# Two transformer blocks with experts: row factors applied late at two steps, narrow FFN ups, second-block projections by rows

## The chip, the cores and the metric

The kernel runs on one core of a Trainium2 chip. The metric is the device time of one execution in microseconds; where several executions are given, their median. The engines have short names in the profile: PE is TensorE (matmuls), DVE VectorE, ACT ScalarE, POOL GpSimd, SP SyncE, whose queue starts the weight transfers.

## What is computed

For 256 tokens of width 1024, all in fp32, two blocks follow one another; x is the residual stream. Cut to the parts that the change touches:

```python
# first block
z = rmsnorm(x, norm1_g) @ w_in + b_in            # attention and a convolution branch follow
x = x + merged @ w_out                           # "wo"
h2 = rmsnorm(x, norm2_g)
up = dwconv(h2 @ w_up) + b;  gate, val = split(up)
x = x + (gelu(gate) * val) @ w_down              # FFN, width 2816
x = rmsnorm(x, norm_f_g)
# second block
h = rmsnorm(x, norm1_gain)
aq, ak, av, mq, mk, mv, mi, mf, mo, gate_a, gate_m = split(h @ w_in)
att = sliding_window_attention(rope(rmsnorm(aq)), rope(rmsnorm(ak)), av)
hm = rmsnorm(mlstm_chunkwise(mq, mk, mv, mi, mf), ml_gain) * sigmoid(mo)
mixed = sigmoid(gate_a) * (att @ w_a) + sigmoid(gate_m) * (hm @ w_m)
x = x + mixed @ w_out                            # "wo2"
q = rmsnorm(x, norm2_gain) @ peer_w_query        # "pq", expert queries
x = x + experts(q, x)                            # 16384 experts, top 16 of 8 heads
```

`rmsnorm(x, g)` is x times g times one factor per token, 1/sqrt(mean(x*x) + eps).

## The kernel before

**Precision.** Every fp32 operand of a matmul is split into a rounded part (h) and a rest (l), and a product is three matmuls: h with h, l with h, h with l.

**Granules.** The weights come in 455 granules of 128 x 1024 numbers. `granule` (L223) starts a 512 KB transfer to a `raw` tile (four of them) on SP's queue, lets ACT round it into `wh` (L238) and DVE subtract the rest into `wl` (L239), three tiles each; then PE reads both. 199 granules are sections of one packed array (`B.sec(name, i)`), 256 are experts.

**Three forms of a granule's matmuls.** `mm_cols` (L255, lines L261 to L263): the weight is stationary, the activations (128 x 256 tokens) move; 24 matmuls of 256 columns, the result has features on partitions. `mm_wide` (L265, L274) moves h and l of the activations side by side: 8 matmuls of 512 and 8 of 256 columns, and `wide_sum` adds the halves with an ACT copy and a DVE add. `mm_rows` (L281, L290 to L292): the activations are stationary, 512 weight columns move; 12 matmuls for the two tiles of 128 tokens, the result has tokens on partitions.

**Norms.** `scaled_cols` (L334) multiplies a tile of tokens by its row factor and by the gain (`nrm`, DVE L341), and `turn` (L353) transposes it on PE in blocks of 128 x 128 (L357) and splits the result into the tiles X that the matmuls read. The row factor needs the whole row: the eviction of the matmul result, a square with sum on ACT, a sum on DVE (L331), a power on POOL (L312). This stands between wo and the FFN (`rows_out`, L679), between the FFN and the second block (L663 to L675, two norms in a row with factors r1 and r3), and between wo2 and pq. There the second half of the columns is done for token tile 0 first, then for tile 1.

**FFN.** For each of 22 slices f two wide up granules fill PSUM banks, a three-tap convolution and gelu run on ACT and DVE, and `down` (L608) adds gh and gl times the third granule to four banks, two f's later; the last downs wait until after the loop, ordered so that half rows end one after the other.

**Second block.** Keys and values (akv), gates (L814), aq and mv are done by rows or cols in `stream1` (L801); mq and mk by cols. Then `drive` runs three generators beside one another: `stream2` (mo, ga2, gm2 by cols, tanh on ACT into so, ta, tb), `attention` (first `qk_norm`, L919, with the rotation on POOL, L936 to L938) and `mlstm` (first `gates`, L854, a scan on DVE). Then ba and bm, the two branch matrices, by cols; their products with the gates are the mixed rows in Y, which wo2 reads. pq by cols gives the expert queries with features on partitions.

**Order.** The program's order is only a first one: a list scheduler sets the order on each engine ahead of time from dependences and its own costs, and each engine then runs its queue in that order. So DVE instructions of the gates and norms stand between wl subtractions.

Of the kernel before, what the change touches and what calls it, by code (L numbers as in the profile page):

```python
# [11 lines left out]
F32 = mybir.dt.float32  # L12
# [39 lines left out]
def _col(v):  # L52
# [4 lines left out]
         ("cb", 4), ("lg", 4), ("lb", 4), ("fw", 132), ("fb", 44), ("mg", 8), ("gb", 1))  # L57
_ROWS = (("n1", D), ("n2", D), ("nf", D), ("m1", D), ("m2", D), ("b_v", 512), ("qg", 64), ("kg", 64),
# [20 lines left out]
def pack(inputs):  # L79
# [105 lines left out]
class Block:  # L185
# [69 lines left out]
    def mm_cols(self, out, w, x, nk, first=True, last=True, off=0):  # L255

        wh, wl = (t[:, off:off + nk * P].rearrange("p (k n) -> p k n", n=P) for t in w)
        xh, xl = x
        mm = self.nc.tensor.matmul
        for k in range(nk):  # L260
            mm(out, wh[:, k], xh[:, k], start=(first and k == 0), stop=False)  # L261
            mm(out, wh[:, k], xl[:, k], start=False, stop=False)  # L262
            mm(out, wl[:, k], xh[:, k], start=False, stop=(last and k == nk - 1))  # L263
# [79 lines left out]

    def warm(self, n):
# [20 lines left out]
def first_block(B, rp):  # L365
    tc, nc, A = B.tc, B.nc, B.A
    with ExitStack() as es:
# [226 lines left out]
        g2 = B.gain(rp, "n2", "gain")  # L594
        X = B.xcol()
        x1 = rows_out(B, rp, "wo", M, x0, 0.5, g2, X, pool,
                      ("qT", "kT", "v", "y", "th", "sig", "oh", "ol"))


    with ExitStack() as es:  # L600
# [3 lines left out]
        late = []  # L604
        acc = [B.bank("at") for _ in range(4)]
# [9 lines left out]

        for f in range(NFF):
# [733 lines left out]
```

## Time and profile before

| | |
|---|---|
| median of 3 runs | 1445.74 us (1445.27 to 1446.1) |
| the profiled execution's own time | 1447.32 us |
| its span, first to last instruction | 1445.5 us |
| mean granted clock of PE in it | 0.993 |
| PE busy | 1423.3 us, 98% of the span |
| DVE, ACT, POOL busy | 1126.8, 766.7, 52.6 us |

By place in the span: first block to the end of wo, 0 to 192 us; FFN to 385; akv and gates to 400; aq, mq, mk, mv to 466; the three generators to 586; ba to 606; bm to 631; wo2 to 652; pq 660 to 682; experts to the end. The times of the rows below are of this one execution. PE's matmuls are pipelined: the duration of one is longer than the distance to the next one's start, so the price of a matmul is read from starts. A granted clock of 1.00 is 2.4 GHz, 0.50 is 1.2 GHz.

### The profile page before, as it was taken

The numbers are of one execution on the slowest core, as the hardware profiler recorded it, in microseconds if no ns is written. First come the engines' busy times: TensorE is split into PE (matmuls) and PEld (weight loads), VectorE is DVE, ScalarE is ACT, GpSimd is POOL, SyncE is SP. The second block draws the span as 40 slices with busy tenths as digits, with TensorE's granted clock in tenths as the row PEclk, the third lists the DMA queues.
The fourth block names the chain that finished last, engine by engine and source line by source line (L and its number), as shares of the span: only waits on it lengthen the run. The fifth ranks groups of instructions, "written<-read, shape, count | busy, mean of one in ns | idle before, by whom it ended". The sixth has DMA issues, their size and how long they took to land.

```text
span 1445.5 us, 24810 instructions
## 1 busy us (share of the span) xinstructions
PE 1423.3 (98%) x9487; PEld 1252.9 (87%) x9487; DVE 1126.8 (78%) x2125; ACT 766.7 (53%) x1225; POOL 52.6 (4%) x97
## 2 busy tenths in 40 slices
PE   8999999999899999999999999999999999999998
PEld 6988978888788988988999999888888888888887
DVE  6997878888797567674997977999969999666665
ACT  5456566667554666454454444555554444455453
POOL 1000000000204000001000000000000000000000
PEclk9999999999999999999999999999999999999999
DMA  7643556556366423474455555555565545555553
GB/s 270 189 137 117 180 168 196 190 187 219 122 188 206 139 96 117 146 242 150 149 174 177 164 191 173 173 164 171 165 211 179 170 168 173 191 191 192 197 193 131
DMA packets 70103, 251.33 MB, mean 174 GB/s; under 512 B 8025, under 2 KB 8417, under 8 KB 69730
## 3 DMA queue, kind: packets, MB, share of 16 engines
q1 hardware_dynamic: 69698, 249.17, 52.3%
q8 instruction: 74, 1.21, 0.3%
q10 hardware_dynamic: 288, 0.59, 0.1%
q14 instruction: 43, 0.35, 0.1%
HBM read 247.63 MB, written 2.11 MB: 173 GB/s over the span
## 4 chain that ended last, share of the span: by engine, by line
PE 91%; DVE 5%; DMA 1%; ACT 1%; issue 1%; POOL 0%; SPq 0%; POOLq 0%; ACTq 0%; DVEq 0%
PE mm L274 19%; PE mm L261 10%; PE mm L262 10%; PE mm L263 10%; PE mm L1293 8%; PE mm L1295 8%; PE mm L1294 8%; PE mm L292 2%; PE mm L291 2%; PE mm L290 2%; PE at L1271 2%; DVE wl L239 2%; PE at L612 1%; PE at L614 1%; PE at L613 1%; DMA raw<-in_ws_dram 1%
## 5 line engine op out<-in xcount | busy, mean ns | idle before, releaser
L239 DVE TENSOR_TENSOR wl<-raw,wh 128x1024 fp32r<-128x1024 f32 x454 | 554.4, 1223 | 159.7 <-ACT wh L238 154.9
L238 ACT ACTIVATE wh<-raw 128x1024 fp32r<-128x1024 f32 (+1 forms) x457 | 479.8, 1051 | 272.6 <-PE mm L262 209.0
L261 PE MATMUL mm<-x,wh 128*128 128x256 f32 x1088 | 312.6, 287 | 1.3 <-ACT wh L238 0.8
L263 PE MATMUL mm<-x,wl 128*128 128x256 f32 x1088 | 310.7, 286 | 2.7 <-DVE wl L239 2.7
L262 PE MATMUL mm<-x,wh 128*128 128x256 f32 x1088 | 311.6, 286 | 0.3 <-DVE x L250 0.2
L274 PE MATMUL mm<-x,wh 128*128 128x512 f32 x864 | 305.2, 399 | 0.0
L274 PE MATMUL mm<-x,wl 128*128 128x256 f32 x864 | 225.0, 281 | 0.0
L261 PEld LDWEIGHTS mm<-x,wh 128*128 128x128 f32 x1088 | 210.4, 193 | 6.5 <-issue 2.9
L263 PEld LDWEIGHTS mm<-x,wl 128*128 128x128 f32 x1088 | 210.3, 193 | 4.4 <-DVE wl L239 3.1
L262 PEld LDWEIGHTS mm<-x,wh 128*128 128x128 f32 x1088 | 210.2, 193 | 3.7 <-issue 2.7
L1293 PE MATMUL mm<-wh,wsh 128*128 128x512 f32 x512 | 201.6, 394 | 0.0
L1295 PE MATMUL mm<-wh,wsl 128*128 128x512 f32 x512 | 199.4, 389 | 0.0
L1294 PE MATMUL mm<-wl,wsh 128*128 128x512 f32 x512 | 199.2, 389 | 0.0
L274 PEld LDWEIGHTS mm<-x,wh 128*128 128x128 f32 x864 | 158.5, 189 | 29.6 <-DVE x L250 0.2
L274 PEld LDWEIGHTS mm<-x,wl 128*128 128x128 f32 x864 | 163.5, 189 | 8.6 <-DVE wl L239 0.2
L249 ACT ACTIVATE wsh<-W 128x256 fp32r<-128x256 f32 x128 | 53.4, 418 | 188.3 <-PE mm L1294 188.0
L1295 PEld LDWEIGHTS mm<-wh,wsl 128*128 128x128 f32 x512 | 96.1, 188 | 20.3
L1294 PEld LDWEIGHTS mm<-wl,wsh 128*128 128x128 f32 x512 | 96.2, 188 | 19.3
L1293 PEld LDWEIGHTS mm<-wh,wsh 128*128 128x128 f32 x512 | 96.2, 188 | 18.9
L250 DVE TENSOR_TENSOR wsl<-W,wsh 128x256 fp32r<-128x256 f32 x128 | 54.2, 424 | 49.4 <-ACT wsh L249 49.3
L278 ACT ACTIVATE W<-mm 128x256 f32<-128x256 f32 x64 | 24.5, 383 | 94.9 <-PE mm L274 94.9
L292 PE MATMUL mm<-wh,x 128*128 128x512 f32 (+1 forms) x160 | 62.0, 387 | 1.3 <-DVE x L250 1.3
(345 smaller groups left out, 1837.4 us busy)
## 6 DMA issues: line engine op xcount, KB each, us to landing
raw<-in_ws_dram SPq DMA_DIRECT2D x199, 512.0 KB, 3.6
raw<-in_pd_dram SPq DMA_DIRECT2D x128, 512.0 KB, 3.5
raw<-in_pu_dram SPq DMA_DIRECT2D x128, 512.0 KB, 3.5
bias<-in_rpb_dram SPq DMA_DIRECT2D x2, 1024.0 KB, 8.5
x<-in_x_dram SPq DMA_DIRECT2D x4, 256.0 KB, 3.6
r_m<-in_rows_dram SPq DMA_DIRECT2D x2, 512.0 KB, 4.7
mb<-negm_d SPq DMA_DIRECT2D x4, 256.0 KB, 5.1
x<-xn SPq DMA_DIRECT2D x2, 512.0 KB, 5.6
```

The lines of the kernel that those rows point to most:

```text
L238: nc.scalar.activation(wh[:, c], raw[:, c], AF.Copy)
L239: eng.tensor_sub(wl[:, c], raw[:, c], wh[:, c].bitcast(F32))
L249: self.nc.scalar.activation(h, src, AF.Copy)
L250: self.nc.vector.tensor_sub(l, src, h.bitcast(F32))
L261: mm(out, wh[:, k], xh[:, k], start=(first and k == 0), stop=False)
L262: mm(out, wh[:, k], xl[:, k], start=False, stop=False)
L263: mm(out, wl[:, k], xh[:, k], start=False, stop=(last and k == nk - 1))
L274: mm(o, a, b, start=(k == 0 and j == 0), stop=(k == 7 and j == 1))
L292: mm(outs[i], xl[:, k0 + k, ts], wh[:, k], start=False, stop=en)
L1293: nc.tensor.matmul(a, wp[0][:, ts], u[0][:, ns], start=(i == 0), stop=False)
L1294: nc.tensor.matmul(a, wp[0][:, ts], u[1][:, ns], start=False, stop=False)
L1295: nc.tensor.matmul(a, wp[1][:, ts], u[0][:, ns], start=False, stop=(i == NE - 1))
```

## The change

Eight things are edited together.

1. Between wo and the FFN and between the FFN and the second block, the activations are multiplied by the gain only (`plain_cols`) and transposed; the row factor is applied to the results. For the FFN it is laid along the free axis (`across`: two matmuls, an ACT copy) and multiplied in the eviction of an up. In the second block it is a scale of ACT's evictions (`full`, `half`) or, for features on partitions, the tile rb again (gates, mq, mk, now evicted on DVE).
2. The ups are 24 narrow matmuls in place of 16 wide ones. Both halves of an f share one bank and one eviction. The first granules of f = 0, 1, 2 are done for the first half of K, then for the second. The FFN's X are two tiles of their own.
3. mo, ga2, gm2, ba, bm and pq use `mm_rows`. hn is multiplied by so before it is transposed; the mixed rows are transposed into Y, 16 blocks; the queries are transposed, 16 blocks.
4. The gain `mg` is a broadcast row, a transfer on SP's queue, instead of a column.
5. pq's first three granules are done for tile 0, then for tile 1.
6. `qk_norm` and `gates` run in a `drive` beside a new generator `stream1b` (mq, mk, mv); their transposes come later, in `qk_cols` and `gate_cols`.
7. The rotation moves from POOL to DVE, the swapped keys from POOL to ACT, y2's scaling from POOL to ACT; akv's evictions go from DVE to ACT.
8. The first granule of aq is done between the akv matmuls of tile 1.

```diff
     def mm_cols(self, out, w, x, nk, first=True, last=True, off=0, k0=0):
...
-            mm(out, wh[:, k], xh[:, k], start=(first and k == 0), stop=False)
+            mm(out, wh[:, k], xh[:, k0 + k], start=(first and k == 0), stop=False)
...
+    def plain_cols(self, pool, src, g, x, k0, i, width=512):
+        for c in range(0, 512, width):
+            ns = slice(k0 * P + c, k0 * P + c + width)
+            y = pool.tile([P, width], F32, tag="nrm", name="nrm", bufs=4)
+            self.nc.vector.tensor_tensor(y, src[:, ns], g[:, ns], op=OP.mult)
+            self.turn(y, x, k0 + c // P, width // P, i)
+    def across(self, pool, rp, r, tag):
...
+        for i in range(2):
+            nc.vector.tensor_copy(w[:, i:i + 1], bc(r[i], P))
+        b = self.bank("at")
+        for i in range(2):
+            nc.tensor.matmul(b[:, i * P:(i + 1) * P], w[:, i], self.ident, start=True, stop=True)
+        rb = pool.tile([P, T], F32, tag=tag, name="rb")
+        nc.scalar.activation(rb, b[:, 0:T], AF.Copy, scale=32.0)
+        return rb
...
+        rb = B.across(pool, rp, r1, "rb")
...
+        ahead = [B.sec("ffn", 3 * f) for f in range(3)]
+        for kh in range(2):
+            for f, w in enumerate(ahead):
...
+                B.mm_cols(ups[f][:, 0:T], w, X, 4, kh == 0, kh == 1, kh * 512, 4 * kh)
         for f in range(NFF):
+            b = ups.get(f) or B.bank("mm")
+            for j in range(2):
+                if j or f not in ups:
+                    B.mm_cols(b[:, j * T:(j + 1) * T], B.sec("ffn", 3 * f + j), X, 8)
...
+            nc.vector.tensor_tensor(u[:, :, 1:T + 1], b.rearrange("p (a t) -> p a t", a=2), bc_at(rb, 1, 2),
+                                    op=OP.mult)
...
-                b = B.bank("mm")
-                B.mm_wide(b, B.sec("ffn", 3 * f + j), X)
-                B.wide_sum(u[:, j, 1:T + 1], b)
...
+                nc.vector.tensor_tensor(x2[i][:, ns], x1[i][:, ns], acc[2 * i + hf], op=OP.add)
+                B.plain_cols(rp, x2[i], g3, X, 4 * hf, i, 256 if hf and i else 512)
...
-            B.scaled_cols(rp, y2, {i: B.power(u, rp, "r3")}, g3, X, 256 if i else 512)
+            r3.append(B.power(u, rp, "r3"))
...
             nc.vector.scalar_tensor_tensor(out[i][:, ns], bs[i], scale, res[i][:, ns], op0=OP.mult, op1=OP.add)
+            if late:
+                B.plain_cols(rp, out[i], g, X2, 4 * nh, i, 256 if nh and i else 512)
...
+            akv(0, 0)
+            akv(1, 0)
+            akv(0, 1)
+            B.mm_rows(qs, aq[0], X, 0, 2, 512, True, False)
+            akv(1, 1)
+            st["rb"] = B.across(pool, rp, r3, "rb")
...
-                    nc.scalar.activation(dst[:, n:n + 2], b.rearrange("p (a t) -> p a t", a=2), AF.Copy)
+                    nc.vector.tensor_tensor(dst[:, n:n + 2], b.rearrange("p (a t) -> p a t", a=2),
+                                            bc_at(st["rb"], 1, 2), op=OP.mult)
...
-                    b = pair(name, n)
-                    nc.scalar.activation(dst[:, n:n + 2], b.rearrange("p (a t) -> p a t", a=2), AF.Tanh, scale=0.5)
...
+                        B.mm_rows(bs, B.sec(name, 4 * nh + gi), X, 2 * gi, 2, 512, gi == 0, gi == 3)
...
+                        nc.scalar.activation(dst[:, i, ns], bs[i], AF.Tanh, scale=half[i])
...
-                    nc.gpsimd.tensor_tensor(t[j], u, w, op=OP.mult)
+                    nc.vector.tensor_tensor(t[j], u, w, op=OP.mult)
...
+        drive((1.0, stream1b()), (0.8, qk_norm()), (0.5, gates()))
         drive((1.0, stream2()), (4.0, attention()), (2.0, mlstm()))
...
+        def second(i, nh, ns, b):
+            t = tb[:, i, ns]
+            nc.vector.scalar_tensor_tensor(t, t, 1.0, b, op0=OP.add, op1=OP.mult)
+            nc.vector.tensor_tensor(t, t, pa[:, i, ns], op=OP.add)
+            B.turn(t, Y, 4 * nh, 4, i)
```

Three places show what the scheduler makes of it. First PE where wo ends and the FFN's ups begin (L290 to L292, in the kernel after L291 to L293, are wo; L357 and L379 transposes; L274 and L262 to L264 ups; L361 the broadcast). Before:

```order
L290 MATMUL mm<-wh,x 128x512
L291 MATMUL mm<-wl,x 128x512
L292 MATMUL mm<-wh,x 128x512
L357 MATMUL at<-ident,nrm 128x128 x12
L274 MATMUL mm<-x,wh 128x512
L274 MATMUL mm<-x,wl 128x256
L274 MATMUL mm<-x,wh 128x512
L357 MATMUL at<-ident,nrm 128x128 x4
```

After, a piece of wo:

```order
L293 MATMUL mm<-wh,x 128x512
L379 MATMUL at<-ident,nrm 128x128 x4
L291 MATMUL mm<-wh,x 128x512
L292 MATMUL mm<-wl,x 128x512
L293 MATMUL mm<-wh,x 128x512
```

After, eleven ups behind wo's end:

```order
L263 MATMUL mm<-xfl,wh 128x256
L379 MATMUL at<-ident,nrm 128x128 x2
L264 MATMUL mm<-xfh,wl 128x256
L379 MATMUL at<-ident,nrm 128x128 x2
L361 MATMUL at<-ident,rw 128x128 x2
L262 MATMUL mm<-xfh,wh 128x256
```

All 16 transposes stood behind wo; now 12 stand between wo's matmuls, and the last four and the broadcast behind the first eleven ups.

Second DVE at the end of the FFN (x and y with numbers are x2 and y2 of one token tile; nrm goes to the transposes). Before:

```order
L663 TENSOR_TENSOR x_3929<-xn,at 128x512 x2
L665 TENSOR_TENSOR y_3930<-x_3929,r_nf 128x512
L331 SCALAR_TENSOR_TENSOR v<-ss 128x1
L663 TENSOR_TENSOR x_3933<-xn,at 128x512
L670 TENSOR_TENSOR u_4011<-ss 128x1
L665 TENSOR_TENSOR y_3934<-x_3933,r_nf 128x512
L671 SCALAR_TENSOR_TENSOR u_4011<-v,u_4011 128x1
L341 SCALAR_TENSOR_TENSOR nrm<-y_3930,pw,r_m_3923 128x512 x2
L663 TENSOR_TENSOR x_3933<-xn,at 128x512
```

After:

```order
L699 TENSOR_TENSOR x_4199<-xn,at 128x512 x2
L350 TENSOR_TENSOR nrm<-x_4199,r_m_2149 128x512 x2
L705 TENSOR_TENSOR y_4200<-x_4199,r_nf 128x512 x2
L251 TENSOR_TENSOR x<-at,x 128x4x128 x2
L699 TENSOR_TENSOR x_4203<-xn,at 128x512
L332 SCALAR_TENSOR_TENSOR v<-ss 128x1
L350 TENSOR_TENSOR nrm<-x_4203,r_m_2149 128x512
```

The product that is transposed (nrm) comes right behind the sum x of its tile, and no longer behind the row's sums and the power.

Third DVE beside the mq and mk matmuls (L239 and L240 are the wl subtractions; L928 to L931 and L1007 to L1012 the head norms; L1017 to L1019 the rotation; L900 the eviction of mk). Before:

```order
L928 TENSOR_TENSOR qk<-qk,rsy 128x1152
L239 TENSOR_TENSOR wl<-raw,wh 128x1024
L930 TENSOR_TENSOR qk<-qk,qg 128x1024
L931 TENSOR_TENSOR qk<-qk,qg 128x128
L305 SCALAR_TENSOR_TENSOR rst<-rsy 128x18
L239 TENSOR_TENSOR wl<-raw,wh 128x1024
```

After:

```order
L240 TENSOR_TENSOR wl<-raw,wh 128x1024
L1007 TENSOR_TENSOR qk<-qk,rsy 128x1152
L900 TENSOR_TENSOR mk<-mm,rb 128x512
L1018 TENSOR_TENSOR qk<-rt 128x18x8
L1019 TENSOR_TENSOR qk<-rt 128x18x8
L1011 TENSOR_TENSOR qk<-qk,qg 128x1024
L1012 TENSOR_TENSOR qk<-qk,qg 128x128
L240 TENSOR_TENSOR wl<-raw,wh 128x1024
```

Between two subtractions there now also stand an eviction and parts of the rotation.

## Rows read from the trace of the kernel before

**Rows 1.** The page: busy time by engine; the chain that ended last
```profile
PE 1423.3 (98%) x9487; PEld 1252.9 (87%) x9487; DVE 1126.8 (78%) x2125; ACT 766.7 (53%) x1225; POOL 52.6 (4%) x97
...
PE 91%; DVE 5%; DMA 1%; ACT 1%; issue 1%; POOL 0%; SPq 0%; POOLq 0%; ACTq 0%; DVEq 0%
```

**Rows 2.** Busy us by stretch: PE, PEld, DVE, ACT, POOL, clock, DMA, GB/s
```profile
426.00:451.00 25.00, 25.00 (x188) 24.00 (x187) 24.83 (x62) 11.32 (x15) 12.33 (x10) 1.00 0.53 169
451.00:466.00 15.00, 15.00 (x68) 12.43 (x67) 6.92 (x7) 7.35 (x8) 3.62 (x7) 1.00 0.78 258
466.00:586.00 120.00, 119.83 (x951) 106.95 (x950) 75.58 (x184) 77.53 (x189) 0.00 (x0) 1.00 0.37 122
```

**Rows 3.** The same of PE alone: busy, granted clock, DMA, GB/s
```profile
196.30:199.70 3.40, 3.40 (x14) 0.50 0.42 152
387.50:394.30 6.80, 5.82 (x27) 0.50 0.12 41
657.10:660.50 3.40, 3.40 (x18) 0.50 0.00 0
```

**Rows 4.** PE timeline, wo to first down: start, duration, operation, idle before
```profile
191.13 0.39 PE L292 MATMUL mm<-wh,x 128*128 128x512 f32 x1
...
194.60 0.44 PE L357 MATMUL at<-ident,nrm 128*128 128x128 f32 x2 [2.21 <-DVE nrm L341]
...
214.92 0.40 PE L612 MATMUL at<-wh,gh 128*128 128x512 f32 x1
```

**Rows 5.** PE timeline from the last downs to the first aq matmul
```profile
377.68 0.50 PE L612 MATMUL at<-wh,gh 128*128 128x512 f32 x1 [1.31 <-ACT gh L249]
...
385.36 1.32 PE L357 MATMUL at<-ident,nrm 128*128 128x128 f32 x8 [1.01 <-DVE nrm L341]
...
388.48 0.58 PE L292 MATMUL mm<-wh,x 128*128 128x256 f32 x1 [1.28 <-DVE x L250]
...
400.39 0.40 PE L290 MATMUL mm<-wh,x 128*128 128x512 f32 x1
```

**Rows 6.** PE timeline at the start of bm and behind wo2
```profile
608.50 0.38 PE L261 MATMUL mm<-mh,wh 128*128 128x256 f32 x1 [0.71 <-ACT mh L249]
...
655.03 0.44 PE L357 MATMUL at<-ident,nrm 128*128 128x128 f32 x2 [2.37 <-DVE nrm L341]
```

**Rows 7.** PE timeline, first and last of runs of one form
```profile
426.15 0.28 PE L261 MATMUL mm<-x,wh 128*128 128x256 f32 x1
...
440.55 0.28 PE L261 MATMUL mm<-x,wh 128*128 128x256 f32 x1
...
451.38 0.39 PE L290 MATMUL mm<-wh,x 128*128 128x512 f32 x1
...
462.26 0.39 PE L290 MATMUL mm<-wh,x 128*128 128x512 f32 x1
...
472.77 1.03 PE L948 MATMUL at<-ident,qk 128*128 128x128 f32 x8
...
473.64 0.27 PE L953 MATMUL at<-ident,qk 128*128 128x128 f32 x1
...
612.26 0.28 PE L261 MATMUL mm<-mh,wh 128*128 128x256 f32 x1
...
626.39 0.28 PE L261 MATMUL mm<-mh,wh 128*128 128x256 f32 x1
```

**Rows 8.** Chain that ended last, one FFN slice: start, duration, what
```profile
217.88 5.60 PE mm L274 x32
```

**Rows 9.** DVE: two groups of 398 to 466 us; one eviction's timeline
```profile
L239 DVE TENSOR_TENSOR wl<-raw,wh 128x1024 fp32r<-128x1024 f32 x26 | 31.7, 1221 | 11.7 <-ACT wh L238 11.7
...
L931 DVE TENSOR_TENSOR qk<-qk,qg 128x128 f32<-128x128 f32 x2 | 0.5, 273 | 0.0
...
191.56 0.69 DVE L695 SCALAR_TENSOR_TENSOR xn<-mm,x 128x512 f32<-128x512 f32 x1 [0.91 <-PE mm L292]
```

More of the change, by code (lines that the diff above doesn't have):

```diff
@@ L253, in xcol, with mm_cols @@
         return Cols(self.xp.tile([P, nk, 2, T], FR, tag="x", name="x"))
-    def mm_cols(self, out, w, x, nk, first=True, last=True, off=0):
+    def mm_cols(self, out, w, x, nk, first=True, last=True, off=0, k0=0):
         wh, wl = (t[:, off:off + nk * P].rearrange("p (k n) -> p k n", n=P) for t in w)
@@ L593, in first_block @@
         B.show("mergedx2", tb)
[L594 to L597, printed above, removed]
+        g2 = B.row_bcast(rp, "n2", tag="gain")
+        X = tuple(fp.tile([P, 8, T], FR, name="xf" + c) for c in "hl")
+        x1, r1 = rows_out(B, rp, "wo", M, x0, 0.5, g2, X, pool,
+                          ("qT", "kT", "v", "y", "th", "sig", "oh", "ol"), late=True)
     with ExitStack() as es:
@@ L707, in rows_out @@
                 evac(i)
+    if late:
+        return out, r
     for i in range(2):
@@ L772, in second_block @@
                                 channel_multiplier=-1)
-        hg = pool.tile([P, 8], F32, name="hg")
-        nc.vector.tensor_scalar(hg, B.col("mg", 0, 8), 0.5, None, op0=OP.mult)
+        hg = B.row_bcast(rp, "mg", tag="gain")
+        nc.gpsimd.tensor_scalar(hg, hg, 0.5, None, op0=OP.mult)
+        rr = pool.tile([P, 2, 2], F32, name="rr")
+        for i in range(2):
+            nc.gpsimd.tensor_scalar(rr[:, 0, i:i + 1], r3[i], 32.0, None, op0=OP.mult)
+            nc.gpsimd.tensor_scalar(rr[:, 1, i:i + 1], r3[i], 16.0, None, op0=OP.mult)
+        full = [rr[:, 0, i:i + 1] for i in range(2)]
+        half = [rr[:, 1, i:i + 1] for i in range(2)]
         qk = pool.tile([P, 2, 18, 64], F32, name="qk")
@@ L929, in qk_norm @@
                 yield
+            kss = []
+            for i in range(2):
                 nc.vector.tensor_tensor(qk[:, i, 0:16], qk[:, i, 0:16], bc_at(qg[:, 0], 1, 16), op=OP.mult)
@@ L1016, in mlstm @@
         def mlstm():
-            yield from gates()
+            yield from gate_cols()
             aT, em = st["aT"], st["em"]
@@ new lines, in branch, with first @@
+        def branch(name, x, done):
+            for nh in range(2):
+                bs = [B.bank("mm"), B.bank("mm")]
+                for gi in range(4):
+                    B.mm_rows(bs, B.sec(name, 4 * nh + gi), x, 2 * gi, 2, 512, gi == 0, gi == 3)
+                for i in range(2):
+                    done(i, nh, slice(nh * 512, nh * 512 + 512), bs[i])
+        def first(i, nh, ns, b):
+            nc.vector.scalar_tensor_tensor(pa[:, i, ns], ta[:, i, ns], 1.0, b, op0=OP.add, op1=OP.mult)
@@ L1086, in second_block @@
+        def second(i, nh, ns, b):
[3 more added lines that the diff above has]
+            B.turn(t, Y, 4 * nh, 4, i)
+        branch("ba", st["O"], first)
         for i in range(2):
             for q in range(2):
[L1088 to L1092 removed]
@@ L1107, in second_block @@
+        branch("bm", M, second)
         B.show("mixedx2", tb)
```

184 lines of the change are left out of this document (101 added, 83 removed).

## The prediction

> **What bounds the kernel now.** I read the page first: TensorE (PE) is busy 98% of the span, and the chain that ended last is PE for 91% of it [rows 1]. So only two things can move the time: how long PE's instructions take in their row, and the few places where PE waits or runs at half clock. The table of busy time by stretch shows which engines stand close behind: in 426 to 451 us VectorE (DVE) is busy for 24.83 of 25 us, in 466 to 586 for 75.58 of 120; PE is full in both [rows 2]. Next the granted clock: it is 1.00 nearly everywhere and 0.50, the 1.2 GHz level, in three stretches that the change touches, of 3.40, 6.80 and 3.40 us [rows 3]. Each follows waits of PE: it idles 2.21 us ahead of 194.60 [rows 4], 1.31, 1.01 and 1.28 ahead of 377.68, 385.36 and 388.48 [rows 5], 2.37 ahead of 655.03 [rows 6]. While the clock is halved, half of the time is lost: 1.7, 3.4 and 1.7 us. Waits and clock at these steps are all that a better order can give: 3.9 us at the first step, 7.0 at the second, 4.1 at the third (waits and lost half added up).
>
> The price of PE's work itself is in the distance between starts. 120 matmuls of the cols form lie between 426.15 and 440.55, so one is 0.1200 us and a granule of 24 is 2.880; with X in tiles of its own (the bm granules) 120 take 612.26 to 626.39, 0.1178, 2.827 a granule. In the rows form 48 lie between 451.38 and 462.26, 0.2267, so a granule of 12 is 2.720. Eight transposes take 472.77 to 473.64, 0.109 each [rows 7].
>
> **The change part by part.** *Rows in place of cols.* mo, ga2, gm2 and pq (32 granules) go from 2.880 to 2.720, ba and bm (16) from 2.827 to 2.720: 32 x 0.160 + 16 x 0.107 = 5.12 + 1.71 = **-6.8** [rows 7]. PE is full there, so all of it is on the path. The Trainium skill ("TensorE: Matmul & The Clock Gate", "Wait — 56ns, not 53.3ns?") speaks against this: it prices a warm matmul at its columns over 2.4 GHz plus about 2.5 ns, so a granule of equal columns would win only 12 x 2.5 = 30 ns, 48 granules 1.4 us (an estimate from that page). By it the term would be -1.4. The trace does not agree: 0.2267 us for 512 columns is 0.443 ns a column, 0.1200 for 256 is 0.469 [rows 7], a wider gap than 2.5 ns a matmul makes; the measurement decides.
>
> *What rows cost back.* The results now have tokens on partitions, so mixed (16) and the expert queries (16) must be transposed: 32 x 0.109 = 3.5. The turns of hn stay, only later. Every block of them is a change of form on PE; I take eight of them at one slot, 0.1: 0.8. Together **+4.3** (3.5 to 5.1).
>
> *FFN ups by cols.* Two wide granules took 5.60 us (x32 in the chain) [rows 8]; 48 cols matmuls from separate tiles take 5.654, +0.054 for each f. 19 of 22 f's are not in the next term: **+1.0**. If the slot is 0.1200 as with the interleaved X, it is 5.76, and the term 3.0; I take 0.1178 since the new X is two tiles, as mh and ml are. On DVE one 128x512 op from PSUM (0.69 at 191.56 [rows 9]) takes the place of two adds, and ACT loses two copies: lighter, not late.
>
> *First late factor.* Before, from the last wo matmul to the first down are 214.92 - 191.13 = 23.79 us [rows 4]: 6 granules, the transposes, the 2.21 wait, the half clock. After, 12 of the 16 transposes lie inside wo, the other 4 and the 2 matmuls of the broadcast after it: 0.23 + 6 x 2.827 + 18 x 0.109 (the 12 counted as well) = 19.2. Waits: the first K half of three granules needs only what is ready, but the order puts the last transposes 11 matmuls behind wo and the broadcast of r right behind them; r of tile 1 needs the eviction (0.69), a square, a sum and a power, which before were most of the 2.21 us wait. PE gets there some 2.3 us after wo, r about 3.3: I take 1.2 for all waits, half of the 2.21. 20.4 against 23.8: **-3.4**. With no wait it is -4.6; with a half clock of 3.40 us behind it -1.7. The first down then waits for gh, which now hangs on one eviction for both halves; the 1.31 at 377.68 [rows 5] is the nearest row for such a wait, nothing is the other end, since PE's order puts ten matmuls of the next up ahead of it: **+0.5**.
>
> *Second late factor.* From the last downs' start to aq is 400.39 - 377.68 = 22.71 us [rows 5]. After, the same work at full clock: the downs 385.36 - 1.01 - 377.68 = 6.7, transposes 16 x 0.109 = 1.7, akv 48 x 0.118 = 5.7, gates 24 x 0.118 = 2.8, the broadcast 0.2, waits 0.7 (my choice, a fifth of the 3.6 of before): 17.8. That would be -4.9. A half clock of 3.40 us costs 1.7 and is about even odds, since three waits in a row become shorter ones (the sums and powers leave the path; adds, gain product, transposes, split stay on it): **-4.0**, ends -6 and -1. aq's first granule is now among the akv matmuls, a cover of 2.7 us for tile 1's transposes; without it the wait of 1.28 comes back.
>
> *mq, mk and norms.* DVE gets four evictions of 0.69 and twelve rope ops of about 0.27 (nearest row 128x128, 273 ns [rows 9]; on GpSimd they held nobody up), +6.0 in a stretch where it has 0.17 of 25 us free [rows 2]. Queued behind them on DVE are the wl subtractions (1.22 each [rows 9]), for which PE waits. Against that, three wl buffers are a lead of up to three granules, 8.2 us, and the gates' scan now stands behind the last mq and mk. Bounds 0 and 5.8; I take **+0.5**, nearer to no wait, since in the same stretch DVE was full before and PE was too.
>
> *Smaller.* bm's first matmuls waited 0.71 for mh [rows 6], now split in the turns: **-0.5**. At pq the first three granules are done tile 0 first, so 3 x 1.36 = 4.1 us of matmuls lie before tile 1's transposes, for which PE waited 2.37 [rows 6]; tile 0's own eviction stays: **-1.2** (-2.5 to +0.5). Transposes of mixed and queries wait for an eviction: **+0.6** (0 to 1.5). The new row of gains and the sinks on SP's queue stand ahead of weight loads; four raw buffers hold up to 4 x 2.72 = 10.9 us of work in hand, behind which two loads hide: 0 (a wait of a load's length, where that cover is gone, falls inside the range). rr and the square sums on GpSimd and ACT, y2's scaling on ACT, ks on ACT: off the path, 0.
>
> Sum: -6.8 + 4.3 + 1.0 - 3.4 + 0.5 - 4.0 + 0.5 - 0.5 - 1.2 + 0.6 = -9.0 us. The profiled execution took 1447.32 us, 1.8 of it outside its span of 1445.5 and 1.6 above the median of 1445.74; the terms are differences, so I take them off the median: **1436.7 us**.
>
> **Rivals.** *The steps keep their waits.* The first step wins 1.9 and the second 1.0: +4.5, 1441.2 us. For: each late factor still has an eviction, a product, a transpose and a split in a row, and the broadcast needs r early. Against: in the new order K halves and aq stand between.
> *VectorE late.* The 5.8 us of DVE comes out on PE between 426 and 455, and a half clock of 6.80 us follows: 5.8 + 3.4 - 0.5 = +8.7, 1445.4 us, the same as before. For: 24.83 of 25 [rows 2]. Against: the lead of three granules, and 6.92 of 15 us busy in the stretch behind [rows 2].
> *Columns alone count.* If form matters only by the number of instructions, wide against cols tells the price: 8 fewer save 2.827 - 2.80 = 0.03, 12 fewer 0.04, 48 granules 1.9 in place of 6.8: 1441.6 us. Against: the rows of 451.38 to 462.26 [rows 7]. The skill's sentence above is this rival; the trace bears it out least.
> *Slower: the clock.* Each new block of transposes or short wait drops the clock: at the first step (3.4), the second (1.7 beyond the half counted), before bm (3.4), at the two turns of mixed (6.8), behind wo2 (1.7), at the queries (3.4): +20.4, 1457.1 us; it is slower than before from four of the six on. Against: 1.00 in 466 to 586 with the transposes of attention in it [rows 2]. The Trainium skill ("TensorE: Matmul & The Clock Gate", "Part 4: PE-mode transpose") says that transposes do not count as PE-busy for the gate in the same way, which speaks for it; the stretch at 1.00 does not agree.
> *Better:* no half clock at either step and no waits: some 5 us less, 1431.7.
>
> **How the numbers follow.** Under 0.2% (2.9 us) a measurement of this kernel can't be told from no change. Forecast 0.60 (0.57 faster, 0.03 same); steps keep waits 0.15 (0.09, 0.06 same); VectorE late 0.10 (0.08 same, 0.02 slower); columns 0.02 (half, half); clock 0.06 (slower); better 0.07 (faster). Faster 0.74, same 0.18, slower 0.08. Range: forecast, kept waits, columns and better hold 0.84; with the ends of the open terms 1431.0 to 1444.5.
>
> **What would show it.** Starts of rows matmuls 0.227 apart in mo to gm2, ba, bm and pq; starts of ups 0.118 apart; first down 20 to 21 us behind the last wo matmul; 17 to 19 us from the last downs to the end of the gates without aq's granule; no wait of PE for wl between 400 and 470; the clock at 1.00 from 466 to 650. The forecast is wrong if the ups stand 0.120 or more apart, if PE waits for wl behind the rope ops, or if 0.50 shows up at a turn.

## The result and the profile after

The changed kernel takes 1437.73 us (median of 9 runs, 1435.48 to 1440.62) against 1445.27 us (median of 9, 1441.93 to 1447.82): ratio 0.9949, 95% interval [0.9941, 0.9957], faster by 7.5 us (6.2 to 8.5). Forecast were 1436.7 us and 9.0 us less, a little more than the interval holds. The profiled execution of the changed kernel took 1435.71 us, 2.0 below its median, that of the kernel before 1447.32, 2.1 above the median of the nine; so the two traces differ by 11.6 us, and some 4 of these are the two executions and not the change. A second profile of the changed kernel, taken in the last experiment, is used beside the first.

The page after, busy time by engine and the chain by engine, beside [rows 1]:

```profile
PE 1417.8 (99%) x9303; PEld 1236.7 (86%) x9303; DVE 1122.4 (78%) x2110; ACT 758.3 (53%) x1191; POOL 40.5 (3%) x86
...
PE 90%; DVE 5%; DMA 2%; issue 1%; ACT 1%; POOL 0%; SPq 0%; ACTq 0%; DVEq 0%; POOLq 0%
```

PE is busy 5.5 us less, in a span 11.8 us shorter: the other 6.3 us are time in which PE did nothing before. Then PE's busy time by stretch (busy, granted clock, DMA share, GB/s): the first step, the second step, the second block up to bm, and bm to the queries (the stretch of the ups, 213 to 372 us, is left out):

```profile
192.00:213.00 21.00, 20.50 (x167) 1.00 0.48 153
...
372.00:397.00 25.00, 24.81 (x153) 1.00 0.30 95
...
397.00:595.00 198.00, 197.76 (x1102) 1.00 0.49 158
...
595.00:676.00 81.00, 78.93 (x385) 1.00 0.57 185
```

The clock is 1.00 in all four; the three stretches at 0.50 of [rows 3] have no counterpart in this execution (the second profile has two of them). The timeline of PE at the first step, beside [rows 4], with wo's first matmul, the inserted transposes' wait, wo's last matmul, the broadcast, the first down:

```profile
167.80 0.39 PE L291 MATMUL mm<-wh,x 128*128 128x512 f32 x1
...
182.12 0.44 PE L379 MATMUL at<-ident,nrm 128*128 128x128 f32 x2 [1.16 <-DVE nrm L350]
...
192.35 0.40 PE L293 MATMUL mm<-wh,x 128*128 128x512 f32 x1
...
195.43 0.38 PE L361 MATMUL at<-ident,rw 128*128 128x128 f32 x1 [0.38 <-DVE rw L358]
...
212.88 0.47 PE L640 MATMUL at<-wh,gh 128*128 128x512 f32 x1
```

192.35 to 212.88 is 20.53 us, where it was 23.79; the 2.21 us wait is now one of 1.16 earlier, in the middle of wo, and one of 0.38. But 20.53 leaves out what went into wo: 12 transposes and the 1.16 us. Counted from wo's first matmul, which before was here,

```profile
169.22 0.39 PE L290 MATMUL mm<-wh,x 128*128 128x512 f32 x1
```

the step takes 45.08 us, where it took 45.70 to the first down at 214.92; ten matmuls of the next up, 1.2 us, now also lie ahead of that down. The second step, beside [rows 5] (last up, start of the last downs, first aq matmul behind the gates):

```profile
371.46 0.28 PE L264 MATMUL mm<-xfh,wl 128*128 128x256 f32 x1
...
376.95 0.50 PE L640 MATMUL at<-wh,gh 128*128 128x512 f32 x1 [0.19 <-ACT gh L250]
...
396.69 0.40 PE L291 MATMUL mm<-wh,x 128*128 128x512 f32 x1
```

396.69 - 376.95 = 19.74 us, and this holds aq's first granule, 2.72: 17.0 where it was 22.7. Last the two places of [rows 6]: bm's first matmul, now without a wait (one of 0.24 follows at 595.77), and behind wo2 the first matmul of the queries, which waits for tile 0 alone:

```profile
594.80 0.50 PE L291 MATMUL mm<-wh,mh 128*128 128x512 f32 x1
...
643.81 0.50 PE L291 MATMUL mm<-wh,x 128*128 128x512 f32 x1 [1.21 <-ACT x L250]
```

By stretches between starts on PE, the three traces compare like this (the forecast's terms summed over the same stretch; a star marks a stretch in which the clock falls to 0.50):

| stretch of PE | before, us | after, first profile | after, second profile | forecast of the difference |
|---|---|---|---|---|
| wo's first matmul to first down | 45.7* | 45.1 | 47.7* | -3.4 + 0.5 |
| first down to last up | 156.5 | 158.6 | 158.6 | +1.0 |
| last up to aq, without aq's granule | 29.0* | 22.5 | 22.6 | -4.0 |
| aq to bm's first matmul, with that granule | 205.5 | 200.8 | 200.8 | -4.7 + 0.5 |
| bm to the first expert score | 81.6* | 81.0 | 82.5* | +1.1 |

### The profile page after: what moved, and what is told of

It reads as the page before. It is cut to its first block, busy times and chain, and to the rows that moved or that the text cites. A ratio compares the mean times of both kernels' runs of the same rounds, so it can differ in the third digit from the quotient of the medians.

```text
span 1433.7 us, 24359 instructions
## 1 busy us (share of the span) xinstructions
PE 1417.8 (99%) x9303; PEld 1236.7 (86%) x9303; DVE 1122.4 (78%) x2110; ACT 758.3 (53%) x1191; POOL 40.5 (3%) x86
## 4 chain that ended last, share of the span: by engine, by line
PE 90%; DVE 5%; DMA 2%; issue 1%; ACT 1%; POOL 0%; SPq 0%; ACTq 0%; DVEq 0%; POOLq 0%
PE mm L275 13%; PE mm L262 9%; PE mm L264 9%; PE mm L263 9%; PE mm L1392 8%; PE mm L1394 8%; PE mm L1393 8%; PE mm L293 5%; PE mm L291 5%; PE mm L292 5%; PE at L1370 2%; DVE wl L240 2%; PE at L640 1%; DMA raw<-in_ws_dram 1%; PE at L641 1%; PE at L642 1%
## 5 line engine op out<-in xcount | busy, mean ns | idle before, releaser
L240 DVE TENSOR_TENSOR wl<-raw,wh 128x1024 fp32r<-128x1024 f32 x454 | 554.3, 1223 | 152.3 <-ACT wh L239 149.1
L239 ACT ACTIVATE wh<-raw 128x1024 fp32r<-128x1024 f32 (+1 forms) x457 | 479.9, 1052 | 279.2 <-PE mm L263 156.9
L264 PE MATMUL mm<-x,wl 128*128 128x256 f32 x832 | 236.3, 284 | 2.7 <-DVE wl L240 2.7
L262 PE MATMUL mm<-x,wh 128*128 128x256 f32 x832 | 237.7, 286 | 0.8 <-ACT wh L239 0.8
L263 PE MATMUL mm<-x,wh 128*128 128x256 f32 x832 | 236.9, 285 | 0.0
L275 PE MATMUL mm<-x,wh 128*128 128x512 f32 x512 | 180.9, 399 | 0.0
L262 PEld LDWEIGHTS mm<-x,wh 128*128 128x128 f32 x832 | 160.2, 193 | 3.7 <-ACT wh L239 1.3
L264 PEld LDWEIGHTS mm<-x,wl 128*128 128x128 f32 x832 | 160.2, 193 | 3.7 <-DVE wl L240 3.1
L263 PEld LDWEIGHTS mm<-x,wh 128*128 128x128 f32 x832 | 160.2, 193 | 2.0 <-issue 1.8
L275 PE MATMUL mm<-x,wl 128*128 128x256 f32 x512 | 132.9, 280 | 0.0
L291 PE MATMUL mm<-wh,x 128*128 128x512 f32 (+1 forms) x288 | 112.0, 389 | 1.2 <-ACT x L250 1.2
L293 PE MATMUL mm<-wh,x 128*128 128x512 f32 (+1 forms) x288 | 112.1, 389 | 0.1
L292 PE MATMUL mm<-wl,x 128*128 128x512 f32 (+1 forms) x288 | 112.0, 389 | 0.0
L275 PEld LDWEIGHTS mm<-x,wh 128*128 128x128 f32 x512 | 93.6, 188 | 17.0
L275 PEld LDWEIGHTS mm<-x,wl 128*128 128x128 f32 x512 | 96.6, 189 | 4.5
```

The costliest lines, as they stand in the source:

```text
L239: nc.scalar.activation(wh[:, c], raw[:, c], AF.Copy)
L240: eng.tensor_sub(wl[:, c], raw[:, c], wh[:, c].bitcast(F32))
L262: mm(out, wh[:, k], xh[:, k0 + k], start=(first and k == 0), stop=False)
L263: mm(out, wh[:, k], xl[:, k0 + k], start=False, stop=False)
L264: mm(out, wl[:, k], xh[:, k0 + k], start=False, stop=(last and k == nk - 1))
L275: mm(o, a, b, start=(k == 0 and j == 0), stop=(k == 7 and j == 1))
```

## The experiments

All times are medians in us beside the kernel before on the same chip (1445.25, 1445.27 and 1445.6 in the three groups). Stretches at 0.50 are read as PE's windows: busy, granted clock, DMA share, GB/s.

**The first late factor undone (e1).**

```diff
-        x1, r1 = rows_out(B, rp, "wo", M, x0, 0.5, g2, X, pool, (...), late=True)
+        x1 = rows_out(B, rp, "wo", M, x0, 0.5, g2, X, pool, (...))
...
-        rb = B.across(pool, rp, r1, "rb")
+        rb = pool.tile([P, T], F32, name="rb")
+        nc.gpsimd.memset(rb, 1.0)
```

> The changed kernel with the first late factor undone: behind wo the rows are multiplied by gain and row factor and then transposed, as before the change; the eviction of the ups multiplies by ones. All else as changed (1437.7 us). Theory (the forecast's first step): 2.2 us of waiting for the factor and a half clock behind it come back, +3.4 us, 1441.1. Rival: only the wait comes back, no half clock, since the K halves follow, +1.5 us, 1439.2. Rival: the broadcast and the waits inside wo of the late form cost as much as they save, 0 us.

Measured: 1440.59, ratio 0.9960 [0.9946, 0.9974], 2.9 us over the changed kernel. PE's timeline there has the old wait again between wo's first matmul and the first down, and the clock falls behind it:

```profile
168.34 0.39 PE L291 MATMUL mm<-wh,x 128*128 128x512 f32 x1
...
193.66 0.33 PE L379 MATMUL at<-ident,nrm 128*128 128x128 f32 x1 [2.20 <-DVE nrm L342]
...
215.97 0.48 PE L641 MATMUL at<-wh,gh 128*128 128x512 f32 x1
```

```profile
194.80:198.20 3.40, 3.40 (x17) 0.50 0.42 128
```

The median is what the first term says (2.9, forecast 3.4 less 0.5 for gh), but the intervals of the two kernels overlap, so that 0 is not excluded. The rows show what the difference hangs on: from wo's first matmul to the first down are 47.6 us here, with a fall; the changed kernel takes 45.1 in its first profile, without one, and 47.7 in its second, with one. So the wait behind wo is gone, but a wait and transposes inside wo take its place; by these traces the late form gains where the clock does not fall behind that wait, and nothing where it does.

**The second late factor undone (e2).**

```diff
-                B.plain_cols(rp, x2[i], g3, X, 4 * hf, i, 256 if hf and i else 512)
...
-            r3.append(B.power(u, rp, "r3"))
+            B.scaled_cols(rp, y2, {i: B.power(u, rp, "r3")}, g3, X, 256 if i else 512)
+            one = rp.tile([P, 1], F32, tag="one%d" % i, name="one")
+            nc.gpsimd.memset(one, 1.0 / 32.0)
+            r3.append(one)
```

> The changed kernel with the second late factor undone: both norms' factors are taken before the transposes, the later scales are one. All else as changed (1437.7 us). Theory by the two profiles (6.3 us between the last down and the end of the gates): +6 us, 1443.7, with a stretch at clock 0.50 of 3 to 7 us. Rival, the forecast's term: +4.0 us, 1441.7. Rival: aq's granule among the akv matmuls hides most of the waits and the clock stays at 1.00, +1.5 us, 1439.2.

Measured: 1443.21, ratio 0.9986 [0.9978, 0.9995], +5.5 us. PE waits for both tiles' products again, and aq's granule does not hide the second; a fall follows. Last up, the two waits, first aq matmul behind the gates:

```profile
370.39 0.28 PE L264 MATMUL mm<-xfh,wl 128*128 128x256 f32 x1
...
384.58 0.33 PE L379 MATMUL at<-ident,nrm 128*128 128x128 f32 x1 [1.31 <-DVE nrm L342]
...
392.16 0.33 PE L379 MATMUL at<-ident,nrm 128*128 128x128 f32 x1 [2.28 <-DVE nrm L342]
...
403.88 0.40 PE L291 MATMUL mm<-wh,x 128*128 128x512 f32 x1
```

```profile
392.70:396.10 3.40, 3.40 (x19) 0.50 0.45 146
```

The term was undersized: the forecast kept half of a fall that the changed kernel does not have there. By the rows the step is worth more than the 5.5 of the medians: from the last up to aq are 33.5 us here and 25.2 in the changed kernel, 8.3 more; but in this kernel the ups, whose code is the same, run faster, 156.6 us from the first down to the last up in place of 158.6 (last section), and that hides 2.0 of it.

**The form of the ups (e3, e8, e7).** Three kernels. First, e3, wide ups with the late factor multiplied on GpSimd:

```diff
-                    B.mm_cols(b[:, j * T:(j + 1) * T], B.sec("ffn", 3 * f + j), X, 8)
...
+                    B.mm_wide(b, B.sec("ffn", 3 * f + j), X)
...
+                B.wide_sum(u[:, j, 1:T + 1], b)
+                nc.gpsimd.tensor_tensor(u[:, j, 1:T + 1], u[:, j, 1:T + 1], rb, op=OP.mult)
```

> The changed kernel with the ups wide again (16 matmuls a granule, ACT copy and VectorE add, then the row factor on GpSimd), in both halves of K for the first three slices. Theory (a cols matmul costs 0.120 us whether X is interleaved or in two tiles, as the profile of the changed kernel shows from 230 us on): 22 x (5.76 - 5.60) = 3.5 us less, 1434.2. Rival, the forecast's step (0.1178): 1.2 us less, 1436.5. Rival: the longer chain from the ups to gh (copy, add, GpSimd) makes TensorE wait, 1438 or more.

Measured: 1457.8, ratio 1.0079 [1.0066, 1.0092]. Then e8, the same with the product on VectorE (`nc.vector` in the last line):

> The changed kernel with wide ups and the late factor multiplied by VectorE behind the add (0.42 us each, 44 of them), in place of GpSimd as in e3. Theory: the chain is short again, VectorE rises from about 82% to 93% of the FFN and still keeps up: 3 us less than the changed kernel, 1434.7. Rival: VectorE at 93% lets the wl subtractions come late and TensorE waits, 1440 or more; then the narrow ups are what makes room for the late factor.

Measured: 1446.32, ratio 1.0003 [0.9994, 1.0012]. Last e7, wide ups and the first factor early, so without any product:

```diff
-        x1, r1 = rows_out(..., late=True)
+        x1 = rows_out(...)
...
-            nc.vector.tensor_tensor(u[:, :, 1:T + 1], b.rearrange("p (a t) -> p a t", a=2), bc_at(rb, 1, 2),
-                                    op=OP.mult)
...
+                    B.mm_wide(b, B.sec("ffn", 3 * f + j), X)
...
+                B.wide_sum(u[:, j, 1:T + 1], b)
```

> The changed kernel with the first late factor undone and the ups wide again, without any multiplication by the factor in their eviction; it differs from e1 in the form of the ups alone (1440.6 us there). Theory (a cols matmul costs 0.120 us in the FFN): 22 x (5.76 - 5.60) = 3.5 us less than e1, 1437.1. Rival, the forecast's step (0.1178): 1.2 less, 1439.4. Rival: the ACT copy and the second add of the wide form cost as much as the matmuls save, 1440.6.

Measured: 1438.23, ratio 0.9948 [0.9935, 0.9961], 2.4 us less than with narrow ups and the same early factor; the intervals of these two overlap, so the reading is in PE's rows. One f of the changed kernel, from its first up to the down behind it:

```profile
265.83 0.28 PE L262 MATMUL mm<-xfh,wh 128*128 128x256 f32 x1
...
271.59 0.40 PE L640 MATMUL at<-wh,gh 128*128 128x512 f32 x1
```

(271.59 - 265.83) / 48 = 0.1200 us. The wide pair in the chain that ended last of the third kernel (start, duration, what):

```profile
232.06 5.61 PE mm L275 x32
```

5.61. So narrow ups cost 0.15 us an f more, not 0.054: 22 f's make 3.3 by these rows, beside the 2.4 of the medians. But in the two kernels that were tried a late factor and wide ups do not go together. With GpSimd in the chain PE waits 12 times at the downs; busy us of PE, PEld, DVE, ACT, POOL in 200 to 338 us follow, of the kernel with GpSimd and then of that with VectorE:

```profile
PE at L641 <- DVE wl L240: 7.6, 12, 0.7
```

```profile
200.00:338.00 138.00, 128.44 (x660) 105.16 (x659) 102.94 (x171) 81.50 (x139) 48.50 (x47) 1.00 0.53 164
```

```profile
200.00:338.00 138.00, 137.10 (x719) 115.70 (x718) 126.30 (x220) 94.18 (x154) 4.17 (x18) 1.00 0.57 183
```

In the first, PE is busy for 128.4 of 138 us: the chain from ups to gh is too long, GpSimd holds it for 48.5 us (in this stretch ScalarE waits 42.2 us for GpSimd's product, and VectorE, on whose queue the wl subtractions stand, 27.9 us for ScalarE). In the second VectorE stands at 126.3 of 138 (113.6 before the change); PE keeps up, but behind the FFN the row factor of the second block comes late, and PE waits for it; that VectorE's load is what makes it late is likely, but not shown:

```profile
400.14 0.58 PE L361 MATMUL at<-ident,rw 128*128 128x128 f32 x1 [5.91 <-DVE rw L358]
```

**The queries by cols again (e4).**

```diff
-        _blocks_a(a["peer_w_query_2"][0], 512),
+        _blocks_b(a["peer_w_query_2"][0]),
...
+        for j in range(2):
+            B.mm_cols(b[:, j * T:(j + 1) * T], B.sec("pq", n + j), X, 8)
+        nc.scalar.activation(qT[:, n:n + 2], b.rearrange("p (a t) -> p a t", a=2), AF.Copy)
```

> The changed kernel with the expert queries by cols again: 24 matmuls a granule, no transposes of queries, tile 0 not first. All else as changed (1437.7 us). Theory by the forecast's terms: +1.3 for the form, +1.2 for the wait behind wo2, -1.7 for the 16 transposes, -0.4 for changes of form, -0.3 for waits: 0 us, 1437.7. Rival: the wait behind wo2 brings a half clock back, +1.7 more, 1439.4. Rival: the transposes cost more than the form, so that undoing gains 1.5 us, 1436.2.

Measured: 1441.88, ratio 0.9969 [0.9955, 0.9984], +4.1 us; the intervals of this kernel and of the changed one just overlap. The old wait behind wo2 is there again, and a stretch of 3.4 us at 0.50 from 651.4 us on:

```profile
649.63 0.30 PE L379 MATMUL at<-ident,nrm 128*128 128x128 f32 x1 [2.46 <-DVE nrm L342]
```

Last bm matmul and first expert score, here, in the first profile of the changed kernel and in its second:

```profile
622.88 0.39 PE L293 MATMUL mm<-wh,ml 128*128 128x512 f32 x1
...
682.01 0.37 PE L1233 MATMUL at<-keys,pq 64*128 64x128 f32 x1
```

```profile
618.29 0.39 PE L293 MATMUL mm<-wh,ml 128*128 128x512 f32 x1
...
675.82 0.37 PE L1247 MATMUL at<-keys,pq 64*128 64x128 f32 x1
```

```profile
622.41 0.39 PE L293 MATMUL mm<-wh,ml 128*128 128x512 f32 x1
...
681.44 0.37 PE L1247 MATMUL at<-keys,pq 64*128 64x128 f32 x1
```

These are 59.1, 57.5 and 59.0 us. The clock falls behind wo2 in the first and the third, and not in the second. So with the fall in both the part is worth 0.1 us, as the theory says; against the first profile it is 1.6, the half clock of the first rival. The 4.1 of the medians is not placed: this execution has a second fall, inside wo, which the part doesn't touch, and four of its seven executions take over 1440 us, where five of eighteen of the changed kernel do. Whether the longer wait behind wo2 makes a fall more frequent, so few do not tell.

**Norms and gates in turn again (e6).**

```diff
-        drive((1.0, stream1b()), (0.8, qk_norm()), (0.5, gates()))
+        for _ in stream1b():
+            pass
...
-                    nc.vector.tensor_tensor(t[j], u, w, op=OP.mult)
+                    nc.gpsimd.tensor_tensor(t[j], u, w, op=OP.mult)
```

> The changed kernel with the norms and gates in turn: stream1b runs before the three generators as in the kernel before, rotation and swapped keys on GpSimd again. All else as changed (1437.7 us). Theory (the forecast's term, and no wait of TensorE in that stretch of the changed profile): -0.5 to 0 us, 1437.5. Rival: the six microseconds more on VectorE cost TensorE's time somewhere, undoing gains 2 to 5 us, 1434. Rival: norms beside the projections are worth something, undoing costs 2 us, 1439.7.

Measured: 1442.31, ratio 0.9981 [0.9972, 0.9990], +4.6 us: the last rival, at more than twice its size. Not in the stretch of mq and mk, but more than 100 us later, inside ba, PE waits and the clock falls for 3.4 us behind it:

```profile
581.68 0.50 PE L292 MATMUL mm<-wl,oh 128*128 128x512 f32 x1 [2.48 <-DVE wl L240]
```

What it waits for is a wl subtraction that stands on VectorE's queue behind the last steps of the mLSTM:

```profile
577.48 1.21 DVE L1156 TENSOR_TENSOR hn<-num,den 128x1024 f32<-128x1024 f32 x1
...
579.21 1.21 DVE L1158 TENSOR_TENSOR hn<-hn,so 128x1024 f32<-128x1024 f32 x1
...
580.41 1.22 DVE L240 TENSOR_TENSOR wl<-raw,wh 128x1024 fp32r<-128x1024 f32 x1
```

The changed kernel had these two steps behind it by then (at 558.9 and 561.2 us). Busy us of PE, PEld, DVE, ACT, POOL in 560 to 583 us, in turn and then as changed:

```profile
560.00:583.00 23.00, 20.52 (x116) 15.48 (x116) 21.26 (x67) 13.22 (x29) 0.00 (x0) 1.00 0.30 95
```

```profile
560.00:583.00 23.00, 22.97 (x118) 17.00 (x118) 12.16 (x20) 15.62 (x39) 0.00 (x0) 1.00 0.51 170
```

VectorE is busy for 21.3 of 23 us in the one and for 12.2 in the other.

**The rows form without the rest (e5, e10)**, with the norms in turn and then beside. The second differs from the first by the `drive` line and the rotation's engine, as above.

```diff
-        drive((1.0, stream1b()), (0.8, qk_norm()), (0.5, gates()))
+        for _ in stream1b():
+            pass
...
+        B.mm_cols(b[:, j * T:(j + 1) * T], B.sec("pq", n + j), X, 8)
...
+        B.mm_wide(b, B.sec("ffn", 3 * f + j), X)
...
+        B.scaled_cols(rp, y2, {i: B.power(u, rp, "r3")}, g3, X, 256 if i else 512)
```

> The changed kernel with all undone but the rows form of mo, ga2, gm2, ba and bm (and aq's granule among the akv matmuls): both factors early, wide ups, queries by cols, norms and gates behind the projections, rotation on GpSimd. Compared with the kernel before (1445.3 us). Theory by the forecast's terms: 24 x 0.160 + 16 x 0.107 = 5.6 less, 16 transposes 1.7 and changes of form 0.4 more, waits 0.2 less: -3.6 us, 1441.7, and up to 1.5 less for aq's granule. Rival, columns alone count: 40 x 0.04 = 1.6 less and 2.1 more, 1445.6.

> As e5 (rows for mo, ga2, gm2, ba and bm; both factors early, wide ups, queries by cols), but with the norms and gates beside the mLSTM projections as in the changed kernel. Theory (in e5 the late end of attention made TensorE wait 2.67 us inside ba, with a half clock behind it): 4.4 us less than e5, 1445.8, about the kernel before. Rival, the forecast's terms as they stand: 1441.7. Rival: the place of the norms has nothing to do with it, 1450 as e5.

Measured: 1450.19, ratio 1.0032 [1.0020, 1.0044], and 1446.24, ratio 1.0008 [0.9999, 1.0017]. The rows form, with aq's granule and the K halves that are left in this kernel, makes it slower by 5 us; the place of the norms gives 4.0 of that back. That the second doesn't come to 1441.7 is not the rows: from aq's start to bm its trace is 4.7 us shorter than before, as in the changed kernel. It loses 3.2 us elsewhere (first step +1.0, last downs +0.6, akv +1.6), where the K halves and aq's granule are still in the code while the factors are early.

**Norms beside the projections, alone, in the kernel before (e11).**

```diff
+        def stream1b():
             for name, dst in (("mq", mq), ("mk", mk)):
...
+        drive((1.0, stream1b()), (0.8, qk_norm()), (0.5, gates()))
         drive((1.0, stream2()), (4.0, attention()), (2.0, mlstm()))
```

> The kernel before with one part of the change alone: norms and gates beside the mLSTM projections, rotation on VectorE, swapped keys on ScalarE; all matmuls in their old form. Compared with the kernel before (1445.3 us). Theory: there TensorE did not wait for attention, since ba by cols began behind its end, so nothing is won: 0 us, 1445.3 (-0.5 to +1). Rival: the part is worth the same 4.6 us alone that undoing it in the changed kernel cost, 1440.7. Rival: VectorE late by its 6 us, 1448 or more.

Measured: 1447.72, ratio 1.0018 [1.0009, 1.0026], slower by 2.1 us. The attention ends 8 us earlier in the trace, 6 counted from the first aq matmul, but with the cols form PE then stands in front of bm, whose operand is multiplied by so on VectorE behind the transposes:

```profile
604.92 0.38 PE L261 MATMUL mm<-mh,wh 128*128 128x256 f32 x1 [1.92 <-ACT mh L249]
...
606.70 0.38 PE L262 MATMUL mm<-ml,wh 128*128 128x256 f32 x1 [1.28 <-DVE ml L250]
```

So this part has no worth of its own; it is what lets ba by rows run without the wait of 2.48 us that it has with the norms in turn.

**The new wait inside wo (e9, and the changed kernel again as a0).** The transposes of wo's first half written nine matmuls later:

```diff
-            if late:
-                B.plain_cols(rp, out[i], g, X2, 4 * nh, i, 256 if nh and i else 512)
+            if late and nh:
+                B.plain_cols(rp, out[i], g, X2, 4, i, 256 if i else 512)
...
+            if late and (i, gi) in ((0, 2), (1, 0)):
+                B.plain_cols(rp, out[((0, 2), (1, 0)).index((i, gi))], g, X2, 0, ((0, 2), (1, 0)).index((i, gi)))
```

> The changed kernel with one thing moved: the gain product and the eight transposes of wo's first half of columns are written nine matmuls (2.0 us) later, behind more of the second half. The changed profile shows TensorE waiting 1.16 us for that product at 182.12; in two of the experiments it waited 2.1 to 2.3 there and the clock fell to 0.50 for 3.4 us behind it. Theory: the wait goes, and with it the fall where there is one, -1.2 to -3 us against the changed kernel, 1435.5. Rival: the wait only moves to the last transposes or the broadcast, 0 us, 1437.7.

> The changed kernel itself once more, on the same chip as e9 to e11: 1437.7 us by all theories; its profile shows whether the clock falls that the other runs have behind the waits at 182 and 643 us come and go with the same program.

Measured: 1436.9, ratio 0.9942 [0.9929, 0.9956], beside 1438.16, ratio 0.9956 [0.9943, 0.9970], for the changed kernel itself. The wait inside wo is down to this:

```profile
189.25 0.33 PE L379 MATMUL at<-ident,nrm 128*128 128x128 f32 x1 [0.51 <-DVE nrm L350]
```

The direction is that of the theory, and it is the fastest kernel of the study by its median, but 1.3 us is within both intervals; that it beats the changed kernel is not shown. The second profile of the changed kernel shows why single executions differ. PE from wo's first matmul over the same place inside wo to the first down, then two windows:

```profile
169.21 0.39 PE L291 MATMUL mm<-wh,x 128*128 128x512 f32 x1
...
184.47 0.33 PE L379 MATMUL at<-ident,nrm 128*128 128x128 f32 x1 [2.07 <-DVE nrm L350]
...
216.95 0.47 PE L640 MATMUL at<-wh,gh 128*128 128x512 f32 x1
```

```profile
185.40:188.80 3.40, 3.40 (x9) 0.50 0.75 247
649.60:653.00 3.40, 3.33 (x8) 0.50 0.31 127
```

The same program that ran at 1.00 from 36.8 us on in the first profile waited 2.07 us instead of 1.16 here, and the clock fell behind this wait and behind wo2, where the wait was the same 1.21 us in both. These two falls, 1.7 us each, the longer wait, 0.9, and 1.0 us lost in the first 64 us make 5.3 of the 5.6 us between the two traces.

## Why the prediction was right, point by point

The time, the direction and the order of size were right; that the sum came within 1.5 us is partly luck. The first step and the ups were forecast to gain 1.9 us together and cost 1.5 by the first profile, 4.1 by the second; the second step was forecast at -4.0 and came at -6.4. These errors have opposite signs and met in the sum.

- **Rows in place of cols, -6.8.** Right where it can be read alone: aq to bm is 4.7 us shorter, as 24 x 0.160 + 8 x 0.107 says. The rival that columns alone count would make this 1.3; it is out.
- **First late factor, -3.4 and +0.5.** Too large by the rows: 0.6 us less from wo's first matmul to the first down in the first profile, 1.8 without the ten matmuls of the next up, and in the second profile, with its fall, nothing is gained. The step took 1.2 us for all waits; there are 1.16 inside wo, 0.38 at the broadcast and 0.12 at the first down, since it placed 12 transposes in wo and asked only what they cost on PE, not when their operand is ready. And it let the half clock go, which is only gone where no fall follows the wait inside wo. Its sign, the first down 20 to 21 us behind wo's last matmul, came true by luck: the 20.4 counted the 12 transposes and not the ten matmuls, the 20.53 hold the ten and not the 12.
- **Narrow ups, +1.0.** Mis-sized: +2.1 from the first down to the last up, 3.3 by the rows of one f. The step that failed is the choice of 0.1178 over 0.1200 "since the new X is two tiles"; the ups 0.120 apart were one of the prediction's own signs of being wrong. The upper bound of the term, 3.0, was nearer. The two tiles are not what sets the slot (last section).
- **Second late factor, -4.0.** Mis-sized: -6.4 by the table; undoing it costs 5.5. The half fall that was kept did not come in either profile of the changed kernel.
- **mq, mk and norms, +0.5.** Wrong sign in the kernel as a whole. PE has no wait there: in 397 to 595 us it is idle for 0.24 us. But the step asked only where VectorE's added work would press, not what the earlier norms bring at the other end: undoing the part costs 4.6 us. The rival "VectorE late" named the mechanism of that loss, at the wrong place and for the wrong kernel: it strikes when the norms are left in turn.
- **What rows cost back, +4.3, and the smaller terms.** Right: bm to the first expert score came 0.6 us shorter in the first profile, without the fall behind wo2 that before had, and 0.9 longer in the second, with it; forecast +1.1. The queries' part is worth 0.1 of it by the rows, forecast next to nothing; the 4.1 us by which the kernel without it was slower are not placed.
- **The slower rival, a fall at every block of transposes,** is out: 32 more transposes, and in both profiles of the changed kernel the clock is 1.00 in the stretches that hold them, except behind a wait of PE (inside wo, behind wo2, both in the second). These two falls are near transposes, which the prediction named as a sign of being wrong; they cost 3.4 us and not 20.4.

So by the table the gain comes from two places: the second late factor, 6.4 us, and aq to bm, 4.7 us, where the rows form saves PE's time only together with the norms' new place (205.3 us with the norms in turn, e5, 200.8 with them beside, e10; 205.5 before). The first late factor and the narrow ups that come with it gain nothing together: from wo's first matmul to the last up are 202.2 us before, 203.7 and 206.3 after, and 202.3 with wide ups and the first factor early, a kernel whose 1438.23 can't be told from the change. Added up by the medians of the experiments, the rows alone +4.9, the norms' place -4.0, the first factor -2.9, the narrow ups +2.4, the second factor -5.5 and the queries -4.1 make -9.2, where -7.5 was measured; of these the first factor, the ups and the queries are not clear of noise.

## What to carry to other kernels

On a kernel whose tensor engine is full, a saving in matmul time comes out only if every engine that feeds the next stage ends earlier by as much: look at what stands in front of the weight splits on VectorE's queue at the end of the stretch that becomes shorter, not only where work is added. A late row factor gains the waits it removes and the clock behind them, as at the second step, but charge it with the waits that the moved transposes bring and with the form that it forces on its consumers: at the first step these took the gain. Price a matmul by the slot that most rows of that form show, and take the worse one where two are seen.

## What the runs showed of the hardware that was not expected

The distance between two cols matmuls is not fixed by the code. The same program, the same lines (the output matmuls of the convolution branch), 42 matmuls apart: first the changed kernel's first profile, then its second.

```profile
161.34 0.28 PE L262 MATMUL mm<-uh,wh 128*128 128x256 f32 x1
...
166.10 0.28 PE L262 MATMUL mm<-uh,wh 128*128 128x256 f32 x1
```

```profile
163.20 0.28 PE L262 MATMUL mm<-uh,wh 128*128 128x256 f32 x1
...
168.15 0.28 PE L262 MATMUL mm<-uh,wh 128*128 128x256 f32 x1
```

The 42 take 4.76 us, 0.1133 each, and 4.95, 0.1179. The ups ran at 0.120 in both; in the kernel with the second factor undone, in which that code is unchanged, at 0.1179 (from the first down to the last up 156.6 us, where the six other traces with narrow ups have 158.6 to 158.7):

```profile
266.21 0.28 PE L262 MATMUL mm<-xfh,wh 128*128 128x256 f32 x1
...
271.87 0.39 PE L639 MATMUL at<-wh,gh 128*128 128x512 f32 x1
```

Three values, 0.1133, 0.1178 and 0.1200, recur; what sets them wasn't found. They are 6.6, 11.1 and 13.3 ns above 256 columns at 2.4 GHz. The 0.2267 of the rows form is 13.4 ns above 512 columns, so that at the slots from which the first term was worked out a matmul costs its columns and some 13 ns, and 12 fewer of them are the 0.160 us of that term. The Trainium skill ("TensorE: Matmul & The Clock Gate", "Wait — 56ns, not 53.3ns?") has about 2.5 ns for this; the rows here do not agree, and the measurement decides.

The clock falls come and go in one program, as the two profiles of the changed kernel show: a 1.21 us wait of PE behind wo2 was followed by 3.4 us at 0.50 in one and by nothing in the other. Inside wo it came behind waits of 1.92, 2.07 and 2.13 us in three traces (e3, a0, e4) and not behind the waits of 0.51 to 1.29 us in the five others with the late form. A wait can be forecast; a fall behind it only as a chance.
